# Moving W_out and the norms of the second token half beside the first half's down projection, and a convolution's LayerNorm across the first half's up projection

## The chip, the cores and the metric

The kernel runs as one program on all 8 cores of one Trainium2 chip. Each core computes 2,048 of the 16,384 tokens, and reads a window of 21 tiles of 128 tokens, because the attention and the convolution look back over 5 tiles. The metric is the device time of the slowest core in microseconds (us). Some executions of any 8-core program fall into a slower state, in which one die has a lower granted TensorE clock; all comparisons here use executions that were not in it, unless the text says so.

Engines are named as in the profile: PE is TensorE, DVE is VectorE, ACT is ScalarE, POOL is GpSimd, SP is SyncE (it mainly issues transfers). 

## The reference, cut to what matters

```python
u = rms_norm(x, norm_mix_pre)
a_val, a_gate, q, k, v = split(u @ w_in)              # 512 columns each
h = a_val * sigmoid(a_gate)
h = causal_depthwise_conv(h, dw_w, dw_b)              # width 31, 512 channels
conv_out = silu(layer_norm(h, ln_g, ln_b))
attn_out = chunked_band_attention(q, k, v, rel_bias)  # 8 heads, 576 keys per 64 queries
x = x + rms_norm(concat(conv_out, attn_out) @ w_out, norm_mix_post)
u = rms_norm(x, norm_ffn_pre)
h = causal_depthwise_conv(u @ w_up, w3, b3)           # width 3, 2 x 2816 columns
gate, val = split(h)
x = x + rms_norm((gelu(gate) * val) @ w_down, norm_ffn_post)
```

All inputs are float32. The kernel multiplies in bf16, so weights have to be cast on the chip.

## The kernel before

A core's program has these stages:

1. A prologue loads w_in as f32 through a ring of eight staging buffers (2 KB rows) and casts it on ACT and DVE; the first projections run.
2. Four attention "slots" (20 exponential steps each). The remaining projections are woven between the steps, and the first half of the convolution lies in the last slot.
3. The second half of the convolution, two LayerNorms, and W_out with its two norms for 17 tiles.
4. The gated FFN in two token halves, H0 and H1: 44 column blocks of the up projection (24 matmuls each), then 8 tiles of the down projection (44 matmuls each).

The convolution is done as matmuls with banded weights (`cwt`, 128 x 20,480 numbers that are mostly zeros), on data that is rearranged by a write to DRAM and a read back (`hd`). Its result is rearranged by a second round trip (`cd`). The instructions of stages 1 to 3 are ordered by a small list scheduler inside the kernel, which uses cost figures of its own; those of the FFN stay in program order on every engine.

The end of the program, with the stage that the change takes apart:

```python
def load_cwt():                      # called in slot 4: f32 in DRAM -> bf16 in SBUF
    for q in range(4):
        S.dma("pool", "cwt%d" % q, lambda q=q: pool.dma_start(out=cwt.ap[:, 8 * q:8 * q + 8, :, :]..., 
              in_=cwt_d[:, 8 * q * 640:(8 * q + 8) * 640]), writes=[cwt[q]], kb=2560, cast=True)

for g in (2, 3, 4, 5):
    slot(g)
load_wo()                            # 8 casting transfers, f32 in DRAM -> bf16 in SBUF
for _, f in conv_units(1):
    f()
conv_norm(0)                         # subtract, multiply (DVE), Silu (ACT), cd out and back, copies
conv_stats(1)
conv_norm(1)
for si in range(6):
    load_wup(si)
for t in range(17 + 5):              # W_out of tile t beside the norms of the tiles before it
    for lag, f in ((5, wo_tp), (4, wo_u), (3, wo_sq2), (2, wo_res), (1, wo_sq1), (0, wo_mm)):
        if 0 <= t - lag < 17:
            f(t - lag)
# ... cut ...
ffn()
```

The prologue's transfers:

```python
def load_w(dst, k, dcol, scol):
    i = wq_i[0] % 8                  # eight staging buffers
    wq_i[0] += 1
    st = wst[i]
    S.dma("sp", "wst%d" % i, lambda: sp.dma_start(out=st.ap, in_=w_in_d[k * 128:(k + 1) * 128, scol:scol + 512]),
          writes=[st], kb=256)
```

The softmax here doesn't subtract the row's maximum and nothing guards it: scores larger than these inputs give would overflow.

## Time and profile before

The median is 881.73 us (880.97 to 883.14). From the head of the profile: the span, and the busy share of PE and of the 16 DMA engines in 40 equal slices of the span (each digit counts tenths, a 9 is 90% or more).

```profile
span 882.3 us, 16351 instructions; the slowest of 8 cores (872.6 to 882.3 us)
...
PE   2898999999997728698999999999999999999996
...
DMA  8996411307977239685999999622399888810323
```

PE is busy 805.6 us in all, 91% of the span. Apart from the start, one gap stands out in its row: the digits 7 7 2 8 6 9 8, from about 265 to 420 us. The same by stage (busy time by window: start and end, length, busy us of each engine with its count of instructions, granted clock, share of the DMA engines, GB/s). The stages are prologue, slots, the stage of convolution, LayerNorm and W_out, then up-H0, down-H0, up-H1, down-H1:

```profile
core 5: us, PE busy (x) PEld busy (x) DVE busy (x) ACT busy (x) POOL busy (x), PEclk, DMA share, GB/s
0.00:80.00 80.00, 56.12 (x435) 29.14 (x436) 39.49 (x94) 42.50 (x80) 15.45 (x45) 0.96 0.85 269
80.00:276.00 196.00, 188.43 (x1828) 104.57 (x1828) 105.04 (x260) 110.98 (x138) 13.75 (x28) 1.00 0.51 77
276.00:407.50 131.50, 94.90 (x688) 58.11 (x689) 94.35 (x136) 94.76 (x191) 5.25 (x6) 0.86 0.62 165
407.50:566.60 159.10, 158.70 (x1081) 104.69 (x1082) 137.97 (x114) 119.46 (x121) 49.05 (x64) 0.99 1.03 120
566.60:646.50 79.90, 79.52 (x378) 36.62 (x376) 25.30 (x21) 12.29 (x20) 7.50 (x18) 1.00 0.28 93
646.50:798.40 151.90, 151.90 (x1033) 100.36 (x1034) 131.52 (x106) 111.09 (x107) 31.70 (x37) 1.00 0.75 74
798.40:882.30 83.90, 76.02 (x353) 34.22 (x350) 26.48 (x22) 11.99 (x19) 5.91 (x16) 0.98 0.28 94
```

The third stage has 131.5 us with 94.9 us of PE work, so 36.6 us of PE idle: that is about all that a better order of this stage can win, as long as PE leads in the stages that take its work over. The slots have 7.6 us of PE idle, and the up and down stages under 0.5 us, except for the 8 us tail.

The chain of waits (start, length, and what the chain passed through) goes through two round trips by way of DRAM, with the LayerNorm between them: `hd` out and back, 13.81 and 10.96 us from 251.78 us on, and then `cd`:

```profile
330.99 12.80 DMA cd<-big
343.91 11.21 DMA big<-cd
```

### The profile page before, as it was taken

The page shows a single profiled execution, that of the slowest core. Times are in us where ns is not written, and L with a number is a line of the kernel's source. Part 1 is how long each engine was busy: PE and PEld are TensorE (multiplying, and loading weights), DVE is VectorE, ACT ScalarE, POOL GpSimd, SP SyncE. Part 2 cuts the span into 40 slices and gives each one's busy share as a digit, 9 for nine tenths or more (in the row PEclk, how much of TensorE's full clock was granted, in tenths as well). Part 3 has the DMA queues.
Part 4 walks back from the last instruction along what each step waited for, and adds up shares of the span by engine and source line. Part 5 has one row for each costly group of instructions (what it writes and reads, how often), then busy time and mean ns, then how long its engine had stood idle before and what let it go on. Part 6 is the DMA issues. An engine that isn't in the chain of part 4 may idle for free.

```text
span 882.3 us, 16351 instructions; the slowest of 8 cores (872.6 to 882.3 us)
## 1 busy us (share of the span) xinstructions
PE 805.6 (91%) x5788; PEld 467.7 (53%) x5788; DVE 560.1 (63%) x750; ACT 503.1 (57%) x673; POOL 128.6 (15%) x213
## 2 busy tenths in 40 slices
PE   2898999999997728698999999999999999999996
PEld 1345445555476703355666666544466666664442
DVE  1666555545453674898988888922258888885232
ACT  3557655455571874798877777611157777773111
POOL 2211100000010020000333333101022222200000
PEclk9999999999998969799999999999999999999999
DMA  8996411307977239685999999622399888810323
GB/s 260 281 282 205 83 12 38 36 1 127 153 103 76 81 100 202 224 272 181 136 124 114 116 115 109 73 96 96 107 147 82 73 78 77 74 13 33 111 96 119
DMA packets 145507, 103.81 MB, mean 118 GB/s; under 512 B 116882, under 2 KB 124434, under 8 KB 144660
## 3 DMA queue, kind: packets, MB, share of 16 engines
q0 software_dynamic: 96704, 36.25, 38.2%
q1 hardware_dynamic: 48148, 65.93, 25.8%
q8 instruction: 47, 0.77, 0.4%
q10 hardware_dynamic: 576, 0.60, 0.3%
q14 instruction: 32, 0.26, 0.1%
HBM read 117.98 MB, written 21.02 MB: 158 GB/s over the span
## 4 chain that ended last, share of the span: by engine, by line
PE 77%; DMA 8%; DVE 6%; issue 4%; ACT 4%; POOL 1%; DVEq 0%; SPq 0%; ACTq 0%; POOLq 0%
PE ps L1036 34%; PE ps L1004 17%; PE ps L615 6%; PE ps L565 4%; PE ps L590 4%; PE ps L601 3%; DMA big<-w_in 2%; PE ps L711 2%; PE ps L746 2%; DMA hd<-big 2%; ACT big L870 2%; DMA cd<-big 1%; DMA big<-cd 1%; DMA big<-hd 1%; DVE big L946 1%
## 5 line engine op out<-in xcount | busy, mean ns | idle before, releaser
L1036 PE MATMUL ps<-big 128*128 128x344 bf16 (+1 forms) x2112 | 313.2, 309 | 1.2 <-DVE big L933 0.5
L1036 PEld LDWEIGHTS ps<-big 128*128 128x128 bf16 x2112 | 205.5, 97 | 108.0 <-issue 1.9
L1004 PE MATMUL ps<-big 128*128 128x512 bf16 x704 | 152.3, 379 | 0.0
L1041 ACT COPY big<-ps 128x1032 f32<-128x1032 f32 x88 | 89.6, 1018 | 82.5 <-DVE big L1045 56.3
L1045 DVE SCALAR_TENSOR_TENSOR big<-big 128x1026 f32<-128x1026 f32 x88 | 113.1, 1285 | 31.7 <-ACT big L1042 28.2
L990 POOL DMA_DIRECT2D big<-w_up x88 | 77.3, 881 | 339.6 <-PE ps L1036 185.6
L1048 DVE SCALAR_TENSOR_TENSOR big<-big 128x1026 f32<-128x1026 f32 x88 | 113.4, 1289 | 9.5 <-DVE big L933 0.4
L1004 PEld LDWEIGHTS ps<-big 128*128 128x128 bf16 x704 | 68.9, 98 | 82.8
L1042 ACT ACTIVATE big<-ps,big 128x1026 f32<-128x1026 f32 x88 | 106.8, 1213 | 0.0
L721 ACT ACTIVATE big<-ps 128x1024 bf16<-128x1024 f32 x80 | 81.8, 1023 | 35.5 <-PE ps L711 20.1
L1012 ACT ACTIVATE big<-ps 128x1024 bf16<-128x1024 f32 x16 | 16.4, 1024 | 129.8 <-PE ps L1004 129.8
L919 PE MATMUL ps<-big 128*128 128x512 bf16 (+1 forms) x272 | 63.9, 392 | 28.9 <-ACT big L870 18.1
L1016 DVE SCALAR_TENSOR_TENSOR big<-ps,big 128x1024 f32<-128x1024 f32 x16 | 20.5, 1284 | 105.7 <-POOL big L501 105.7
L615 PE MATMUL ps<-big 128*128 128x512 bf16 (+1 forms) x320 | 62.0, 339 | 0.5 <-DVE big L623 0.5
L919 PEld LDWEIGHTS ps<-big 128*128 128x128 bf16 (+1 forms) x272 | 26.3, 99 | 61.0 <-issue 33.7
L1059 DVE TENSOR_TENSOR big<-big 128x1026 bf16<-128x1026 bf16 x44 | 53.8, 1222 | 0.7 <-PE ps L1036 0.4
L565 PE MATMUL ps<-big 128*128 128x512 bf16 x168 | 43.5, 413 | 5.8 <-ACT big L493 4.8
L1056 ACT ACTIVATE big<-big 128x1026 bf16<-128x1026 f32 x44 | 46.5, 1057 | 0.4 <-DVE big L1048 0.4
L498 POOL TENSOR_SCALAR big<-big 128x1 f32<-128x1 f32 x37 | 7.7, 208 | 255.1 <-ACT big L1012 174.6
L590 PE MATMUL ps<-big 128*128 128x512 bf16 (+1 forms) x192 | 39.3, 354 | 1.0 <-DVE big L593 0.5
L615 PEld LDWEIGHTS ps<-big 128*128 128x128 bf16 x320 | 25.8, 97 | 26.3 <-issue 1.3
L727 DVE TENSOR_TENSOR big<-big 128x512 bf16<-128x512 bf16 (+1 forms) x80 | 29.4, 368 | 8.9 <-ACT big L721 4.3
(97 smaller groups left out, 796.6 us busy)
## 6 DMA issues: line engine op xcount, KB each, us to landing
big<-w_up POOLq DMA_DIRECT2D x88, 256.0 KB, 6.2
big<-xw SPq DMA_DIRECT2D x37, 512.0 KB, 6.1
big<-w_in SPq DMA_DIRECT2D x40, 256.0 KB, 8.5
h1s<-big SPq DMA_DIRECT2D x16, 512.0 KB, 3.7
big<-h1s SPq DMA_DIRECT2D x16, 512.0 KB, 4.5
out<-big SPq DMA_DIRECT2D x16, 512.0 KB, 3.1
big<-w_down POOLq DMA_DIRECT2D x22, 256.0 KB, 7.5
big<-cwt POOLq DMA_DIRECT2D x4, 1280.0 KB, 25.0
```

The costliest lines, as they stand in the source:

```text
L565: S.mm(lambda k=k: pe.matmul(b.ap, lhsT=ut.ap[:, k, j * 128:(j + 1) * 128], rhs=Wv.ap[:, k, :], start=(k == 0), stop=(k == 7)), reads=[ut[ ...
L590: S.mm(lambda k=k: pe.matmul(b.ap[:, :N], lhsT=Wk.ap[:, k, c * 128:(c + 1) * 128], rhs=ut.ap[:, k, :N], start=(k == 0), stop=(k == 7)), re ...
L615: S.mm(lambda k=k: pe.matmul(b.ap[:, :n], lhsT=Wa.ap[:, k, col:col + 128], rhs=ut.ap[:, k, n0:N], start=(k == 0), stop=(k == 7)), reads=ut ...
L721: S.op("act", lambda: act.activation(out=p_.ap, in_=s_.ap, func=AF.Exp), reads=[s_], writes=[p_, DH["exps"]], n=1024)
L919: S.mm(lambda k=k, half=half, l_=l_: pe.matmul(pp.ap[0:n, half, :], lhsT=l_, rhs=Wo.ap[:, k, half * 512:(half + 1) * 512], start=(k == 0), ...
L990: S.dma("pool", "wup%d" % (si % 8), lambda: pool.dma_start(out=wring[si % 8].ap, in_=w_up_v[:, :, cbk * 128:(cbk + 1) * 128]), reads=[coT[ ...
L1004: S.mm(lambda f=f, half=half, i=i, pdv=pdv: pe.matmul(pdv[:, half * 512:(half + 1) * 512], lhsT=actb.ap[:, f, i * 128:(i + 1) * 128], rhs= ...
L1036: S.mm(lambda k=k, t=t, n_=n_: pe.matmul(pu.ap[:, t, 0:n_], lhsT=wb.ap[:, k, :], rhs=u2T.ap[:, k, b0 + 342 * t:b0 + 342 * t + n_], start=( ...
L1041: S.op("act", lambda: act.copy(out=xs.ap, in_=pu.ap[:, :, 0:344]), reads=[pu], writes=[xs], n=1032)
L1042: S.op("act", lambda: act.activation(out=ta.ap, in_=pu.ap[:, :, 2:344], func=AF.Identity, scale=fdw.ap[:, cbk, 2:3], bias=fdw.ap[:, cbk, 3 ...
L1045: S.op("dve", lambda: dve.scalar_tensor_tensor(out=tB.ap, in0=xs.ap[:, :, 1:343], scalar=fdw.ap[:, cbk, 1:2], in1=ta.ap, op0=ALU.mult, op1 ...
L1048: S.op("dve", lambda: dve.scalar_tensor_tensor(out=ta.ap, in0=xs.ap[:, :, 0:342], scalar=fdw.ap[:, cbk, 0:1], in1=tB.ap, op0=ALU.mult, op1 ...
```

## The change

The intent is to dissolve the third stage. The W_out steps of the first token half and the first half's LayerNorm go into the attention slots. The second half's LayerNorm is spread in small pieces over the column blocks of up-H0, and the second half's W_out (tiles 9 to 16) goes beside down-H0, where DVE and ACT are idle. To free SBUF and to avoid table switches, the normalized activations `u2T` hold one token half only, Silu becomes a tanh form, Sqrt becomes integer and Newton steps on DVE, and the banded weights no longer stay in SBUF: they are cast once, DRAM to DRAM, and streamed twice through a ring of three pieces. W_out is cast DRAM to DRAM too. The core of the diff, cut:

```diff
+    cwb = nc.dram_tensor("cwb", [128, 32 * 5 * 128], BF16).ap()
+    wob = nc.dram_tensor("wob", [D, D], BF16).ap()
 ...
+        def cast_cwt(p):
+            S.dma("pool", "cwb%d" % p, lambda: pool.dma_start(out=cwb[:, p * 2560:(p + 1) * 2560], in_=cwt_d[:, p * 2560:(p + 1) * 2560]),
+                  writes=[DH["cwb"][p]], kb=1280, cast=True)
+        def load_cwt(i):
+            p = i % 8
+            S.dma("sp", "cwt%d" % (i % 3), ... out=cwr[i % 3], in_=cwb[:, p * 2560:(p + 1) * 2560], reads=[DH["cwb"][p]] ...)
+        def cast_wo():
+            for i in range(2):
+                S.dma("pool", "wob%d" % i, lambda i=i: pool.dma_start(out=wob[i * 512:(i + 1) * 512, :], in_=w_out_d[i * 512:(i + 1) * 512, :]),
+                      writes=[DH["wob"][i]], kb=2048, cast=True)
 ... in the prologue, behind the last load of w_in in program order:
+        for p in range(8):
+            cast_cwt(p)
+        cast_wo()
 ... in the loop of the up projection:
+                if H == 0:
+                    k, m = si // 4, si % 4
+                    if si < 32:
+                        (lambda: ln1.mul(k), lambda: [ln1.affine(k, i, "act") for i in (0, 1)],
+                         lambda: [ln1.affine(k, i, "act") for i in (2, 3)], lambda: ln1.tanh(k))[m]()
+                    if m == 0 and 0 < si <= 32:
+                        ln1.out(k - 1)
+                    if si == 32:
+                        ln1.cross()                      # cd out and back
+                    if si >= 37:
+                        for f in turns[2 * (si - 37):2 * (si - 36)]:
+                            f[1]()                       # ACT copies of what cd brought back
 ... in the down projection:
+            for i in range(8):
+                if H == 0 and i < 7:
+                    wo_mm(9 + i)
+                    wo_x(10 + i)
+                    if i:
+                        wo_tp(8 + i)
+                if i:
+                    epi(i - 1)
 ...
+                if H == 0:
+                    for f in (wo_ev, wo_res, wo_sq2, wo_u) if i < 7 else ():
+                        f(9 + i)
+                part(i, 0, 18)                           # 36 of the tile's 44 down matmuls
+                if H == 0 and i == 0:
+                    for f in turns[14:]:
+                        f[1]()
 ... the program's end:
-        load_wo()
-        for _, f in conv_units(1):
-            f()
-        conv_norm(0)
-        conv_stats(1)
-        conv_norm(1)
-        (the loop over 17 W_out tiles)
+        (woven into slots 2 to 5: conv_units, conv_stats, LayerNorm 0, W_out steps of tiles 0 to 8)
```

`cast_cwt` and `cast_wo` read inputs and write a DRAM tensor that nobody has touched, so they wait for nothing.

## The prediction

> **What bounds it now.** The table of engine busy time by 20 us windows (slowest core, span 882.3 us) shows four stages. (a) 0 to 80 us: DMA share 0.76 to 0.96, the loads of w_in set the pace. (b) 80 to about 276 us, attention woven with the projections: PE 97 to 100% busy, VectorE and ScalarE near 55%. (c) 276 to 407 us: PE busy only 5 to 14 us of 20 in four windows (300 to 360) and clock 0.71 to 0.86. The chain of waits names why: hd DMA out and back 13.8 + 11.0 us, LayerNorm on ACT/DVE, cd DMA 12.8 + 11.2 us, then W_out at 3.9 us a tile, 272 matmuls whose tile rate DVE and ACT set. (d) 407.5 to 882: two halves of up (159, 152 us) and down (76 us), PE-bound, plus a 8 us tail.
>
> **Removed.** Stage (c) as a stage. Its PE work from 276 on (rest of conv and its statistics about 25 us, W_out 16 x 3.45 us, transposes) moves elsewhere; the four exposed round trips, about 49 us, and the Silu/Sqrt table switches go.
>
> **Moved.** First-half W_out (9 steps, about 32 us of PE), conv 18 us and statistics 17 us go into the attention slots. I sum PE work there (projections 125, attention 45, conv, statistics, W_out) to about 237 us; DVE and ACT work, with the durations of before, to about 180 each. The slots stay PE-led; at 93% they last about 255 us, against 327 from 80 to 407. Up-H0 gains per four column blocks (13.9 us) about 1.3 us of DVE (87% to 97%) and 2.5 us of ACT (75% to 93%): I allow 4 us of PE stall. Down-H0 gains 8 x (3.45 + 0.45) = 31 us of PE, little else, since DVE (25% busy) and ACT (11%) are idle there. Up-H1, down-H1 and the tail stay 153 + 84.
>
> Sum: 80 + 255 + 4 (drain) + 157 + 109 + 1 + 153 + 84 = 843 us.
>
> **Added, and my main doubt.** The conv weights are now cast DRAM to DRAM (10.5 MB read) and W_out too (4.2 MB). These POOL DMAs depend on nothing, so they should be issued in the first 15 us, into the stage that is DMA-bound. The Trainium skill, "DMA: Bandwidth & Descriptors", section "Issuing engines are not separate DMA queues", says that all issuing engines share the same 16 DMA engines; this trace agrees: the hd write issued beside the cast of cwt at 202 us took about 36 us instead of a median 8.5. The cast of 5 MB there took about 35 us at DMA share above 0.8. Casts at the start can delay w_in by 0 to 40 us. I take 13 us as the middle of an uneven distribution: about 856 us.
>
> **Predicted: 856 us, 8 in 10 between 832 and 882; faster by over 2% 0.60, within 2% 0.35, slower 0.05.**
>
> **What would show it.** No window with PE under 50% after the prologue; first up matmul near 339 to 370 us; down-H0 near 107 us and down-H1 near 76; up-H0 not above 160; DMA share near 1 in the first 100 us and the first attention exp later than 80 us if my doubt is right; only about two activation table loads.
>
> **What would make it wrong.** Casts that share gently (then 840) or starve w_in fully (then 880). Fixed order: a late hd or cd round trip stalls PE in the slots. Only two generic PSUM banks serve W_out, its transposes and the projections. Tanh beside the tanh-GELU in up-H0: if they need different tables, each switch costs 1.28 us as measured here (skill page "ScalarE: Activation LUTs", section "Table sets", warns of switches), 16 times, about 20 us. DVE at 97% in up-H0 could slip more than 4 us.

## More of the kernel before

PE's own timeline shows where it stood still (start, length, line, instruction; brackets hold the idle time before an instruction and what ended it):

```profile
276.86 1.76 PE L819 MATMUL ps<-big 128*128 128x128 bf16 x15 [2.40 <-DMA big<-hd]
...
326.02 18.98 PE L919 MATMUL ps<-big 128*2 128x512 bf16 x80 [18.15 <-ACT big L870]
...
360.03 5.12 PE L919 MATMUL ps<-big 128*128 128x512 bf16 x16 [10.75 <-DVE big L933]
```

PE waited only 2.40 us for `hd`, because attention and convolution work ran beside that trip. The two long waits, 28.9 of the 36.6 us, are one that the profile puts down to ACT's Silu in the LayerNorm (line 870), and one that begins during the way back of `cd` (343.91 to 355.12 us) and ends after the copies of what it brought.

One more view, because the change meets it: the DMA queues in the first 80 us (packets, MB, share of the time of 16 engines) and the loads of w_in (count, KB each, median us from issue to landing). `q1` is SP's queue, `q0` is POOL's.

```profile
q1 hardware_dynamic: 10080, 21.25, 83.0%
q0 software_dynamic: 288, 0.07, 0.9%
...
big<-w_in SPq DMA_DIRECT2D x40, 256.0 KB, 8.5
```

The prologue is bound by SP's loads: they take 83% of all the DMA time that there is.

## The result, and the profile after

The kernel after takes 947.35 us (946.42 to 947.47), against 881.78 us for the kernel before in the same rounds: the ratio is 1.074, with a 95% interval of 1.072 to 1.076. It is 7.4% slower. (Ratios are the mean time of one kernel's fast runs over that of the other's in the same rounds, so they differ a little from the ratio of the medians.)

The head of the profile after, with the same lines:

```profile
span 946.3 us, 16431 instructions; the slowest of 8 cores (937.6 to 946.3 us)
...
PE   0031999989999998979999996999989999999996
...
DMA  8998984566037468427999998453329877840332
```

The gap in PE's row near 300 us is gone, as intended. A larger one has opened at the start: four slices of 23.7 us at 0, 0, 3 and 1 tenths. The windows by stage (prologue up to the first exponential of the attention, slots, up-H0, down-H0, up-H1, down-H1):

```profile
core 2: us, PE busy (x) PEld busy (x) DVE busy (x) ACT busy (x) POOL busy (x), PEclk, DMA share, GB/s
0.00:140.00 140.00, 56.41 (x388) 28.60 (x394) 34.17 (x78) 41.34 (x80) 21.03 (x50) 0.84 0.94 198
140.00:419.40 279.40, 256.22 (x2337) 152.08 (x2367) 167.68 (x342) 160.38 (x250) 49.53 (x119) 0.96 0.51 122
419.40:591.90 172.50, 162.58 (x1081) 105.69 (x1082) 141.33 (x126) 134.06 (x159) 48.96 (x63) 0.96 0.94 113
591.90:709.50 117.60, 111.14 (x557) 51.91 (x566) 56.59 (x62) 41.17 (x81) 18.35 (x41) 1.00 0.39 136
709.50:862.20 152.70, 152.65 (x1032) 101.05 (x1034) 131.61 (x106) 111.26 (x107) 32.41 (x37) 1.00 0.72 77
862.20:946.30 84.10, 75.61 (x345) 33.98 (x350) 26.45 (x22) 12.00 (x19) 6.33 (x16) 0.97 0.26 88
```

The difference of the two profiled spans, 64.0 us, splits exactly into three parts. In the kernel before, the first exponential starts at 78.2 us. (The slowest core is core 5 before and core 2 after.)

| stage | before | after | difference |
|---|---|---|---|
| up to the first exponential | 78.2 | 140.0 | +61.8 |
| from there to the first up matmul | 329.3 | 279.4 | -49.9 |
| FFN | 474.8 | 526.9 | +52.1 |

Single cores differ by some us within a run: before, their first exponential starts at 72.9 to 78.2 us. The medians of the eight cores give differences of +64.8, -52.9 and +50.0 us, so the picture is the same.

The prologue lost almost as much as the whole kernel did. But the table says a second thing: even with the old prologue, the moved work would have won 49.9 us in one place and paid 52.1 us in another. Of these 52.1 us, 31.6 are PE work that now stands in down-H0 (PE busy 111.14 against 79.52 us). Up-H0 got no matmuls (1,081 records in both), yet its PE busy time grew by 3.9 us: the granted clock was 0.91 and 0.75 in the stretches 419 to 440 and 560 to 580 us, the second of which holds a long wait, and 0.99 to 1.00 in the others. The rest is mostly waiting.

The chain of waits after begins with one long stretch of w_in loads and of SP's queue waiting to issue more loads (lines 500 and 485 issue those of w_in and x):

```profile
4.36 28.49 DMA big<-w_in
33.73 13.27 SPq L500
...
60.16 19.57 SPq L485
```

The DMA queues and issues of the first 80 us after:

```profile
q0 software_dynamic: 1517, 7.31, 77.4%
q1 hardware_dynamic: 1778, 4.30, 20.5%
...
big<-w_in SPq DMA_DIRECT2D x16, 256.0 KB, 40.1
```

Before, POOL's queue took 0.9% of the DMA time here and SP's 83%. Now POOL's takes 77.4% and SP's 20.5%. SP moved 4.30 MB instead of 21.25 MB, and a w_in load took 40.1 us instead of 8.5. POOL's part of the timeline (start, length, line, instruction) shows when the casts were issued:

```profile
3.12 1.58 POOL L846 DMA_DIRECT2D cwb<-cwt  x3
...
11.59 1.00 POOL L985 DMA_DIRECT2D wob<-w_out  x2
```

The timeline has all ten (five of them cut here) issued by 13 us, although they stand behind the loads of w_in in the program text. That text is only the order within an engine, and POOL had nothing else to do.

### The profile page after: what moved, and what is told of

Read it like the earlier page. It is cut to its first block, busy times and chain, and to the rows that moved or that the text cites. A ratio compares the mean times of both kernels' runs of the same rounds, so it can differ in the third digit from the quotient of the medians.

```text
span 946.3 us, 16431 instructions; the slowest of 8 cores (937.6 to 946.3 us)
## 1 busy us (share of the span) xinstructions
PE 814.6 (86%) x5731; PEld 473.3 (50%) x5788; DVE 557.8 (59%) x734; ACT 500.2 (53%) x692; POOL 176.6 (19%) x326
## 4 chain that ended last, share of the span: by engine, by line
PE 59%; DVE 12%; DMA 9%; issue 7%; SPq 6%; ACT 4%; POOL 2%; DVEq 0%; ACTq 0%; POOLq 0%
PE ps L1183 23%; PE ps L1112 10%; PE ps L638 6%; PE ps L610 3%; SPq L500 3%; DMA big<-w_in 3%; PE ps L585 3%; PE ps L1028 3%; SPq L485 3%; DVE big L1192 3%; DVE big L1195 2%; PE ps L624 2%; PE ps L865 2%; PE ps L734 2%; DMA big<-xw 2%
## 5 line engine op out<-in xcount | busy, mean ns | idle before, releaser
L1183 PE MATMUL ps<-big 128*128 128x344 bf16 (+1 forms) x2112 | 318.0, 312 | 9.1 <-ACT big L1189 8.6
L1183 PEld LDWEIGHTS ps<-big 128*128 128x128 bf16 x2112 | 207.5, 99 | 118.7 <-issue 11.3
L1112 PEld LDWEIGHTS ps<-big 128*128 128x128 bf16 x704 | 68.0, 97 | 81.7
L745 ACT ACTIVATE big<-ps 128x1024 bf16<-128x1024 f32 x80 | 80.5, 1024 | 44.0 <-PE ps L770 22.1
L518 POOL TENSOR_SCALAR big<-big 128x1 f32<-128x1 f32 (+1 forms) x54 | 16.0, 296 | 292.1 <-ACT big L537 130.1
L638 PE MATMUL ps<-big 128*128 128x512 bf16 (+1 forms) x311 | 61.6, 344 | 2.4 <-DVE big L646 1.4
L1028 PE MATMUL ps<-big 128*128 128x512 bf16 (+1 forms) x262 | 61.4, 381 | 2.6 <-DVE big L1045 1.1
L521 POOL TENSOR_TENSOR big<-big 128x1 f32<-128x1 f32 x71 | 48.6, 685 | 54.6 <-DVE big L1045 47.2
L547 PE MATMUL ps<-big 128*128 128x128 bf16 x168 | 14.8, 240 | 48.4 <-DVE big L593 25.0
L757 POOL MEMSET big<- 64x128 bf16 x64 | 14.0, 218 | 170.7 <-ACT big L745 133.1
L585 PEld LDWEIGHTS ps<-big 128*128 128x128 bf16 x168 | 17.2, 107 | 55.9 <-issue 41.8
```

The lines of the kernel that those rows point to most:

```text
L585: S.mm(lambda k=k: pe.matmul(b.ap, lhsT=ut.ap[:, k, j * 128:(j + 1) * 128], rhs=Wv.ap[:, k, :], start=(k == 0), stop=(k == 7)), reads=[ut[ ...
L638: S.mm(lambda k=k: pe.matmul(b.ap[:, :n], lhsT=Wa.ap[:, k, col:col + 128], rhs=ut.ap[:, k, n0:N], start=(k == 0), stop=(k == 7)), reads=ut ...
L745: S.op("act", lambda: act.activation(out=p_.ap, in_=s_.ap, func=AF.Exp), reads=[s_], writes=[p_], n=1024)
L1028: S.mm(lambda k=k, half=half, l_=l_, b=b: pe.matmul(b.ap[0:n], lhsT=l_, rhs=Wo.ap[:, k, half * 512:(half + 1) * 512], start=(k == 4), stop ...
L1112: S.mm(lambda f=f, half=half, i=i: pe.matmul((PU[1] if i % 2 else PD).ap[:, half, :], lhsT=actb[f].ap[:, i * 128:(i + 1) * 128], rhs=Wd[f] ...
L1183: S.mm(lambda k=k, t=t, n_=n_: pe.matmul(pu.ap[:, t, 0:n_], lhsT=wb.ap[:, k, :], rhs=u2T.ap[:, k, 342 * t:342 * t + n_], start=(k == 0), s ...
```

## The experiments

The first theory was that the casts are the whole loss: they hold the DMA engines while w_in should arrive. The rival was that the loss is made of the fixed order in the FFN and of busier slots, with the casts a side matter.

### e1: the kernel before, with the ten casts and nothing else

The casts write two DRAM tensors that nothing reads.

```diff
--- before
+        for p in range(8):
+            S.dma("pool", "cwb%d" % p, lambda p=p: pool.dma_start(out=cwb[:, p * 2560:(p + 1) * 2560], in_=cwt_d[:, p * 2560:(p + 1) * 2560]),
+                  writes=[DH["cwb"][p]], kb=1280, cast=True)
+        for i in range(2):
+            S.dma("pool", "wob%d" % i, lambda i=i: pool.dma_start(out=wob[i * 512:(i + 1) * 512, :], in_=w_out_d[i * 512:(i + 1) * 512, :]),
+                  writes=[DH["wob"][i]], kb=2048, cast=True)
         late = [Wa[(7, 0)]]
```

> The kernel before plus only the ten early DRAM-to-DRAM casts, whose results nobody reads. Theory A (the casts hold the DMA engines for about 63 us in a stage that is bound by DMA): first attention exp moves from 78 us to about 135 to 142 us and the total from 882 to about 940 to 950 us. Theory B (the new order and buffers of the prologue delay it, the casts slip in between): total within 10 us of 882.

Measured: 947.8 and 948.3 us, ratio 1.0756 (1.0722 to 1.0789). Four of its six runs fell into the slow state, the profiled one among them, so of its trace only the start and the undisturbed cores are used. On the slowest core the first exponential began at 143.5 us, and the DMA queues of the first 80 us read like those of the kernel after:

```profile
q0 software_dynamic: 1516, 7.28, 76.2%
q1 hardware_dynamic: 1778, 4.30, 22.8%
```

Cores 0 to 3, whose die was not slowed, start their first exponential at 139.1 to 141.0 us and take 473.2 to 474.9 us for the FFN, as in the kernel before, so the delay arises in the prologue and nothing is added later.

What follows: the casts alone, added to the old kernel, cost about 66 us, which is all of the loss. The rest of the change is then worth about nothing (947.35 against some 948 us), which agrees with the table above (-49.9 and +52.1). Neither theory was the whole of it: the casts make the loss, and the fixed order and the moved work eat the gain.

### e2: the kernel after, with the casts held back until w_in is loaded

```diff
--- after
         for p in range(8):
-            cast_cwt(p)
-        cast_wo()
         late = [Wa[(7, 0)]]
+        for p in range(8):
+            cast_cwt(p, late)        # reads=late: waits for the last cast weight of w_in
+        cast_wo(late)
```

> The changed kernel with the ten casts held back until the last w_in weight is in place (about 72 us). Theory A: first exp back at 78 to 85 us; but the casts then take their 63 us of DMA time inside the first attention slot, so the conv weights come at about 140 us and the hd round trip is slow: total 885 to 915 us. Theory B: first exp stays near 140 us, total above 940 us.

Measured: 938.41 us, ratio 1.0665 (1.0596 to 1.0735). The first exponential came at 76.6 us again, but the first up matmul only at 413.2 us: of 63 us won in the prologue, 6 were left. The total lies between the two ranges that were expected. The timelines of ACT and PE show one place where most of the 63 us went:

```profile
146.85 1.06 ACT L537 ACTIVATE big<-big 128x1024 bf16<-128x1024 f32 x1 [53.66 <-DMA big<-xw]
...
148.63 5.04 PE L638 MATMUL ps<-big 128*128 128x512 bf16 x15 [51.76 <-ACT big L642]
```

PE stood still for 51.76 us in the middle of the first slot. It waited for ACT (line 642), and ACT, which works in program order, stood for 53.66 us before the norm of a tile of x (line 537) whose load had not landed. That load (512 KB) was issued at 87.06 us and took 59.7 us; the 32 KB write of `hd`, issued just before it at 86.25 us, took 59.4 us. In this stretch (72 to 145 us) POOL's queue took 86.8% of the DMA time. So the casts take their time from whatever transfers run beside them; to move them only chooses the victim.

### e3: the kernel after, casting directly to SBUF

The ring is filled straight from the f32 weights by casting transfers, as the kernel before did, so the weights are read twice; W_out likewise. There is no DRAM-to-DRAM transfer.

```diff
--- after
-        for p in range(8):
-            cast_cwt(p)
-        cast_wo()
 ... in load_cwt:
-            S.dma("sp", ... in_=cwb[:, p * 2560:(p + 1) * 2560]), reads=[DH["cwb"][p]], ...)
+            S.dma("pool", ... in_=cwt_d[:, p * 2560:(p + 1) * 2560]), ... kb=1280, cast=True)
 ... in load_wo:
-                S.dma("sp", ... in_=wob[k * 128:(k + 1) * 128, :]), reads=[DH["wob"][k // 4]], ...)
+                S.dma("pool", ... in_=w_out_d[k * 128:(k + 1) * 128, :]), ... kb=512, cast=True)
```

> The changed kernel without the staging in DRAM: conv weights and W_out are cast straight into SBUF, each conv weight twice, when their buffers come free. Theory A: first exp at 78 to 85 us, total 880 to 900 us, so no better than before, because 20 us in the slots, 15 in the first up and 8 in the first down stay lost. Theory B: total above 940 us.

Measured: 913.8 us (three runs), ratio 1.0359 (1.0317 to 1.0401). The first exponential came at 74.4 us and the first up matmul at 390.1 us. The total is above the 880 to 900 us that were expected: the slots became longer, which the expectation had not counted. Half of the loss is gone without any DRAM-to-DRAM cast; what is left is the FFN, 523.4 us on the profiled span and so 48.6 more than before, and slots of 315.7 us, in which POOL's queue took 30.2% of the DMA time (74 to 314 us), most of it to cast the mostly empty weights twice. That the casts made the slots longer was not tested apart; the longest single wait of PE in them is 11.9 us.

### e4 and e5: the two waits in the FFN

The kernel after has two waits that come from the fixed order. At the end of up-H0, ACT's copies of what `cd` brings back ("turns") stand in ACT's order before the data is there. ACT waits, and PE waits for ACT to drain PSUM. The timeline of the kernel after, ACT and PE:

```profile
571.74 1.15 ACT L974 COPY big<-big 128x256 bf16<-128x256 bf16 x2 [8.62 <-DMA big<-cd]
...
575.05 16.83 PE L1183 MATMUL ps<-big 128*128 128x344 bf16 x96 [8.12 <-ACT big L1189]
```

In down-H0 every tile's transposes (`wo_tp`, line 1084) stand before the tile's own down matmuls and wait for a chain of norms (ACT, POOL, DVE line 1074) of the tile before, while ACT cannot go on before it has copied those transposes out of PSUM (line 1090), which holds up the squares of the next tile's norms behind it:

```profile
635.46 1.29 DVE L1074 SCALAR_TENSOR_TENSOR big<-big 128x1024 bf16<-128x1024 f32 x1 [2.92 <-POOL big L521]
...
636.89 0.61 PE L1084 MATMUL ps<-big 128*128 128x128 bf16 x8 [0.96 <-DVE big L1074]
...
637.59 1.01 ACT L1090 COPY big<-ps 128x1024 bf16<-128x1024 bf16 x1 [3.75 <-PE ps L1084]
```

The loop closes over PE, DVE and ACT in 14.4 us per tile, where PE has 13.4 us of work.

e4 put the copies later, across the down tiles 0, 2 and 4, and was not run: the check refused it, with 66 values that are no numbers; the buffer that the copies read starts at the same SBUF address as one of the output tiles (129732), which is written from tile 1 on (this is read from the program, not tested).

> The changed kernel with two orders mended in the FFN: only 4 of the 16 turns of conv output stay in the first up (at its end), 12 go into the first down; and each transpose of W_out comes behind the down projection of its tile, not in front of it. Theory C (the first up lost 8 us to a wait of ACT on the cd read and 2 to 4 us to ACT overload by the turns, the first down 7 us to an in-order loop over transpose, ACT and DVE): first up 172 to 160-163 us, first down 117.6 to 109-111 us, total about 931 us. Rival D (DVE at 95% in the first up and the added PE work in the first down set those times): both stages within 2 us, total 945 us or more.

e5 keeps the copies within the buffer's life: 4 of the 16 in the last two column blocks, 12 in down tile 0. And the transposes go behind the tile's first 36 down matmuls.

```diff
--- after
-                    if si >= 37:
-                        for f in turns[2 * (si - 37):2 * (si - 36)]:
+                    if si >= 42:
+                        for f in turns[2 * (si - 42):2 * (si - 41)]:
 ...
-                    for f in turns[14:]:
+                    for f in turns[4:]:
 ...
-                    if i:
-                        wo_tp(8 + i)
 ...
                 part(i, 0, 18)
+                if H == 0 and 0 < i < 7:
+                    wo_tp(8 + i)
```

> The changed kernel, casts untouched, with two orders mended in the FFN: 4 of the 16 turns of conv output stay at the end of the first up, 12 go into the first tile of the first down; each transpose of W_out comes behind the down projection of its tile, not in front of it. Theory C (the first up lost 8 us to ACT waiting for the cd read and a few to the turns, the first down 7 us to an in-order loop over transpose, ACT and DVE): first up from 172 to 160-164 us, first down from 118 to 109-112 us, total 929 to 934 us. Rival D (DVE at 95% in the first up, and the PE work added to the first down, set those times): both within 2 us, total 945 us or more.

Measured: 939.89 us, ratio 1.0647 (1.0622 to 1.0673). Up-H0 fell from 172.5 to 166.8 us, and down-H0 from 117.6 to 113.5 us with a period of 13.4 us per tile, PE's own work. But the step from up-H0 to down-H0 now held a wait, for the first four copies, which were issued so late that they themselves ended late:

```profile
587.19 5.08 PE L1028 MATMUL ps<-big 128*128 128x512 bf16 x12 [4.86 <-ACT big L974]
```

The wait comes before the first down matmul, so the 166.8 us of up-H0, taken up to that matmul, contain it. Both stages and the total ended above the ranges expected (160 to 164, 109 to 112, 929 to 934 us). So the two waits are real, and together worth about 7.5 us as mended here, after the loss of 4.9 us to a new wait. They are about a ninth of the loss, not its main part.

### e6 and e7: no casts at all

If the casts are too dear in any place, the weights must come in some other way. `cwt` holds each of its numbers among fifteen zeros. e6 sends the numbers without the zeros (1,280 per partition instead of 20,480, and a 16 x 16 mask), lets DVE multiply them out in slot 2, and stores the bf16 pieces to the same DRAM tensor; the ring is unchanged. W_out is cast straight to SBUF, as before the change. No arithmetic moves to the host; the same numbers arrive in another layout.

```diff
--- after
-    cwt_d = dr("cwt", [128, 32 * 5 * 128])
+    cws_d = dr("cws", [128, 32 * 5 * 8])
+    msk_d = dr("msk", [128, 16])
 ...
+        def build_cwt(p):
+            t = cst[p % 2]
+            for a in range(0, 160, 40):
+                S.op("dve", lambda a=a: dve.tensor_tensor(
+                    out=t.ap[:, a:a + 40, :], in0=cws.ap[:, p * 160 + a:p * 160 + a + 40].unsqueeze(2).to_broadcast([128, 40, 16]),
+                    in1=mskb.ap.unsqueeze(1).to_broadcast([128, 40, 16]), op=ALU.mult), ...)
+            S.dma("sp", ... out=cwb[:, p * 2560:(p + 1) * 2560], in_=t ...)
```

> The changed kernel without any early cast: the banded conv weights are built on VectorE from their 1/16 of nonzero numbers (the host passes the same numbers without the zeros), stored to DRAM by the hardware queue in the first attention slot, and W_out is cast straight into SBUF. Theory A (the early casts cost 62 us and nothing else in the prologue does): first exp at 75 to 82 us, first up matmul at 355 to 370 us, total 883 to 897 us, so the rest of the change is worth nothing to -2%. Theory B: first exp near 140 us, total above 940 us. Should the slots turn out limited by DVE, 22 us more of it would push the first up past 370 us.

Measured: 890.62 us, ratio 1.0089 (1.0021 to 1.0158). First exponential 72.3 us, first up matmul 362.1 us. The casts are out of the way and 57 us are back. The slots became 10.4 us longer than in the kernel after (289.8 against 279.4); it would fit that the building, 32 DVE instructions in the first slot and the wait of the convolution for them, costs about that much.

e7 adds e5's two orders, and moves the attention's memsets, which the change had sent to POOL, back to DVE.

```diff
--- e6
+        (the edits of e5)
-        S.op("pool", lambda m0=m0: pool.memset(p_...
+        S.op("dve", lambda m0=m0: dve.memset(p_...
```

> e6 with the FFN orders of e5, and with the attention memsets back on VectorE. If the stage effects add: e6 minus 15 to 18 us from the FFN, 866 to 880 us in all, faster than before by 0.5 to 2%. Memsets: if the hand-over DVE to POOL to PE (DVE waits 15.7 us for POOL memsets in the slots) delays the attention chain, the time from first exp to first up is 3 to 10 us shorter than in e6; if PE sets the slots, it is equal within 2 us.

Measured: 879.93 us, ratio 0.9978 (0.9924 to 1.0032): a tie with the kernel before. The FFN begins 45.7 us earlier than there (361.8 against 407.5). Up-H0 is 7 us longer and down-H0 34 us longer, so little remains. The memsets made no clear difference: the slots went from 289.8 to 288.2 us on the slowest cores, while the cores of one run spread over 284.2 to 290.5 us in e6.

### e8 and e9: two attempts on the slots

e8 gives every second building piece to POOL and puts the first four copies at column blocks 40 and 41. e9 also moves the first convolution later in its slot, so that PE should not wait for it.

```diff
--- e7
-                    if si >= 42:
-                        for f in turns[2 * (si - 42):2 * (si - 41)]:
+                    if si in (40, 41):
+                        for f in turns[2 * (si - 40):2 * (si - 39)]:
 ...
-                S.op("dve", lambda a=a: dve.tensor_tensor(
+                e, en = (("dve", dve), ("pool", pool))[p % 2]
+                S.op(e, lambda a=a, en=en: en.tensor_tensor(
--- e9 also
-                         (conv_units(0), 0.6, 0.85), ... (one(lambda: conv_stats(0)), 0.9, 1.0)]
+                         (conv_units(0), 0.72, 0.95), ... (one(lambda: conv_stats(0)), 0.98, 1.0)]
```

> e7 with two small changes: the first four turns of conv output come two column blocks earlier in the first up, so that they are done when the first W_out matmul of the first down wants them (e7 waited 4.5 us there), and every second piece of the conv weights is built on POOL, since DVE was 80% busy in the first attention slot of e7 and POOL 13%. Expected: wait before the first down gone (-4 us), time from first exp to first up from 288 to 280-286 us; total 868 to 876 us, faster than before by 0.7 to 1.6%. If POOL work slows DVE beside it, the slots stay at 288 us and the total at 875 us.

> e8 with the first conv 10% of a slot later, so that the hd round trip it waits for (4.1 us in e7) has landed, and its statistics later with it. Theory: waits of PE on DMA in the slots fall by 4 us and the total to 864 to 872 us. Rival: the LayerNorm chain of the first half is the tighter limit, so a later conv moves its cd round trip and W_out back and the total rises by 3 to 10 us.

Measured: e8 876.73 us, ratio 0.9941 (0.9910 to 0.9971); e9 877.74 us, ratio 0.9958 (0.9931 to 0.9985), no different from e8. Both missed their expectations: e8's slots were to fall to 280 to 286 us, and e9 was to take 864 to 872 us. In e8 the slots took 296.9 us on the slowest core; the median of its cores is 288.9 us, against 284.9 in e7, with overlapping spreads, so the split did not shorten them, and how much it lengthened them is not clear. The groups of instructions show one thing against the split (line, engine, operation, shapes, count; busy us and mean ns; idle time before and what ended it):

```profile
L853 POOL TENSOR_TENSOR big<-big 128x640 bf16<-128x640 f32 x16 | 24.4, 1556 | 9.8 <-DMA cwb<-big 7.9 <-DMA big<-msk 1.8
L853 DVE TENSOR_TENSOR big<-big 128x640 bf16<-128x640 f32 x16 | 16.9, 1106 | 2.7 <-DMA cwb<-big 2.2 <-DMA big<-msk 0.5
```

A piece takes 1,556 ns on POOL, and DVE's own pieces took 1,106 ns beside it, against 810 ns when DVE worked alone (e12 below).

### e10 and e11: what in a cast is dear

e10 is e1 with only the two casts of W_out. e11 is e1 with all ten casts, but with destinations cut so that a packet is 640 bytes (conv weights) or 512 bytes (W_out) instead of 5,120 and 32,768.

```diff
--- e1, for e10
-        for p in range(8):
-            S.dma("pool", "cwb%d" % p, ...)
--- e1, for e11
-    cwb = nc.dram_tensor("cwb", [128, 32 * 5 * 128], BF16).ap()
-    wob = nc.dram_tensor("wob", [D, D], BF16).ap()
+    cwb = nc.dram_tensor("cwb", [64, 128, 320], BF16).ap()
+    wob = nc.dram_tensor("wob", [4, D, 256], BF16).ap()
```

> The kernel before plus only the two early casts of W_out (in the trace of e1 their 32 KB packets took 18 us of all 16 DMA engines, those of the conv weights 43). Theory A (delay = DMA engine time of the casts): first exp from 78 to 94-100 us, total 898 to 904 us. Rival (a fixed cost of any early cast on that queue, or of its order): near 940 us, or under 888 us.

> e1 with the same ten casts and bytes, but rows cut to 320 and 256 numbers, so that packets have 640 and 512 bytes in place of 5,120 and 32,768. Theory A1 (each DMA engine takes packets of the two queues in turn, so the queue with the larger packets gets the larger share): w_in gets about half of the time, first exp between 100 and 130 us where e1 had 143.5. Theory A2 (the casts come first whatever their packets, or the sum of work alone counts): first exp at 140 us or later, total 940 us or more.

Measured, e10: 901.8 us (two runs), ratio 1.0227 (1.0195 to 1.0259); first exponential at 94.5 us, 16.3 later than before. POOL's queue in its first 80 us:

```profile
q0 software_dynamic: 384, 2.16, 23.6%
```

The casts of W_out are 64 packets of 32 KB, each 4.51 us long, which is 64 x 4.51 / 16 = 18 us of all 16 engines. The delay was 16.3 us on the slowest cores and 19.7 us in the medians of the eight. In the trace of e1 the conv weights' casts are 1,024 packets of 672 ns, which is 43 us of 16 engines. Both together are 61 us, and the kernel after starts its first exponential 61.8 us late (64.8 us in the medians). So the size of the loss is plain DMA work: in this stage, which is bound by the DMA engines, each us of cast was about a us of delay, within a tenth. The 5 MB of `cwt` did not look like 43 us of work, because a plain 2,048-byte packet of w_in takes 107 ns in the trace of before, 19 bytes per ns, where a casting DRAM-to-DRAM packet of 5,120 bytes makes 7.6. (These are the bytes written; a cast from f32 to bf16 reads twice as many.) The kernel before casts the same `cwt` straight into SBUF, and there it took 31.4 us of 16 engines (57.0% of the stretch from 195 to 250 us), in slots that PE leads: so the change made this cast dearer, and put it where DMA is the limit.

Measured, e11: 939.5 us (two runs), ratio 1.0655 (1.0622 to 1.0688); first exponential at 124.8 us, against 143.5 in e1. Its queues in the first 80 us:

```profile
q1 hardware_dynamic: 6514, 13.11, 60.6%
q0 software_dynamic: 6047, 3.70, 40.6%
```

With small packets POOL's queue gets 40.6% instead of 76.2%, though it holds the same transfers. In this pair of runs the size of the packets set how the two queues shared the engines. The first exponential is as theory A1 expected. But the total moved by only 8 us: the cast work that was held back ran into the first slot instead (the DMA share is 1.01 from 125 to 152 us, and the slots took 336.1 us against 327.8 in e1, medians of the cores). The work is the cost, and the share only dates it.

### e12 and e13: the best version

e12 is e7 with the first four copies at column blocks 40 and 41 (as in e8, but with all building on DVE). e13 also makes bf16 copies of the numbers and the mask first, in the hope that DVE multiplies bf16 faster.

```diff
--- e7, for e12
-                    if si >= 42:
-                        for f in turns[2 * (si - 42):2 * (si - 41)]:
+                    if si in (40, 41):
+                        for f in turns[2 * (si - 40):2 * (si - 39)]:
--- e12, for e13
+        S.op("dve", lambda: dve.tensor_copy(out=cwh.ap, in_=cws.ap), ...)
+        S.op("dve", lambda: dve.tensor_copy(out=mskh.ap, in_=mskb.ap), ...)
-                    in0=cws.ap..., in1=mskb.ap...
+                    in0=cwh.ap..., in1=mskh.ap...
```

> e8 without the building on POOL (its POOL pieces took 1.56 us each beside 0.81 on DVE, and its time from first exp to first up rose from 288 to 297 us), so e7 with only the four turns earlier. Expected: the 4.5 us wait before the first down gone, slots 286-290 us, total 873 to 877 us, ratio 0.990 to 0.996.

> e12 with the conv weights built from bf16 copies: if DVE is faster on bf16 with repeated operands (the attention multiply of 512 bf16 took 0.42 us where 512 f32 took 0.69), each build step falls from 0.81 to 0.4-0.6 us, DVE gives back 7 to 12 us in the first attention slot, and the total is 3 to 8 us below e12. If the repeated operand keeps DVE at its slow rate, both are equal within 2 us.

Measured: e12 873.66 us, ratio 0.9910 (0.9889 to 0.9930); e13 871.95 us (five runs), ratio 0.9889 (0.9840 to 0.9939). What e13 hoped for did not come: the building runs no faster in bf16, and the two are equal within 2 us, the other outcome that was named. The groups of e12 and of e13:

```profile
L852 DVE TENSOR_TENSOR big<-big 128x640 bf16<-128x640 f32 x32 | 24.4, 810 | 2.8 <-DMA cwb<-big 2.6
```

```profile
L854 DVE TENSOR_TENSOR big<-big 128x640 bf16<-128x640 bf16 x32 | 24.4, 808 | 2.6 <-DMA cwb<-big 2.6
```

Both are about 1% faster than the kernel before, with an interval that excludes equality. e12's stages, from its profile: first exponential 72.7 us, first up matmul 362.5, down-H0 524.3, up-H1 635.7, end 872.4. Its FFN takes 509.9 us, 35.1 more than before, and 33.5 of that is PE busy time, 31.5 in down-H0, to which the work was moved. The long waits in the FFN are gone: up-H0 has 1.7 us of PE idle left, down-H0 0.4.

## Why the prediction was wrong, point by point

It said 856 us and "faster"; the result was 947.35 us, far outside its range. Its sum, term by term (the profiled span was 946.3 us; the two add up to a miss of 90.3 us):

| term | predicted | measured | miss |
|---|---|---|---|
| prologue with casts | 80 + 13 | 140.0 | +47.0 |
| slots and drain | 255 + 4 | 279.4 | +20.4 |
| up-H0 | 157 | 172.5 | +15.5 |
| down-H0 | 109 + 1 | 117.6 | +7.6 |
| up-H1, down-H1, tail | 153 + 84 | 236.8 | -0.2 |

**The step that failed: "I take 13 us as the middle of an uneven distribution".** The mechanism was right: the casts depend on nothing, go out in the first 15 us, and share the DMA engines with the loads of w_in. The Trainium skill, "DMA: Bandwidth & Descriptors", section "Issuing engines are not separate DMA queues", says that transfers of all issuing engines run on the same 16 DMA engines; the trace agrees (POOL's queue 77.4%, SP's 20.5% of those engines). The size was wrong. The prediction had costed the cast of 5 MB at about 35 us from the trace of before, left W_out's casts without a figure of their own, and then averaged between "shares gently" and "starves". In a stage with a DMA share of 0.85 there was little to share: the delay had to be nearly the whole DMA time of the casts, measured at 61 us from their packets, and the whole range of "0 to 40 us" was too low. e1, e10 and the packet times show this. (The 35 us were those of a cast into SBUF; into DRAM it took 43.) Even "starve w_in fully (then 880)" was 67 us under the result. It is not the only error that reversed the sign: with the casts alone mis-sized the sum is 843 + 60 = 903 us, and with the other terms alone mis-sized it is 856 + 43 = 899 us. Either is slower than the kernel before.

**"I sum PE work there ... to about 237 us".** PE was busy 256.2 us in the slots, and at the measured 92% (the prediction had 93%) that makes 279.4. The groups of the slots of the kernel after show which terms were missing:

```profile
L770 PE MATMUL ps<-big 128*128 128x65 bf16 x632 | 31.5, 197 | 3.1 <-DVE big L781 2.2 <-DVE big L751 0.8
L734 PE MATMUL ps<-big 64*128 64x128 bf16 (+3 forms) x252 | 25.6, 315 | 5.1 <-ACT big L745 5.1
...
L547 PE MATMUL ps<-big 128*128 128x128 bf16 x96 | 7.7, 226 | 0.8 <-DVE big L705 0.4 <-DVE big L793 0.3
L1084 PE MATMUL ps<-big 128*128 128x128 bf16 (+1 forms) x72 | 6.1, 233 | 1.2 <-DVE big L1042 0.5 <-DVE big L1045 0.4 <-DVE big L1074 0.2
L789 PE MATMUL ps<-big 128*128 128x128 bf16 x48 | 4.8, 225 | 2.0 <-DVE big L793 1.6 <-DVE big L874 0.2
```

The attention (lines 734 and 770) takes 57.1 us where the sum had 45, and the transposes (547, 1084 and 789), 18.6 us, were not in it at all. (Groups overlap: in this stage they add up to 279.7 us, 23.5 more than PE's busy time. So the 12.1 and 18.6 us cannot be set one for one against the 19.2 us that the sum lacked; the groups show which terms were short, not by how much each.) The table of windows would have given it without a sum of parts: 188.43 + 94.90 us of PE work from 80 to 407.5 us, less the 31 us that go to down-H0, is 252.

**"I allow 4 us of PE stall" in up-H0.** The allowance was for DVE and ACT being fuller. What cost most was order: ACT stood for 8.62 us before data that `cd` had not yet brought, and PE for 8.12 us behind it; besides, the same matmuls were busy 3.9 us longer, at a lower granted clock. The warning "a late hd or cd round trip stalls PE" was in the prediction, but for the slots and with no number. e5 and e12 mend it: 172.5, 166.8 and 161.8 us.

**Down-H0.** The PE work was right (31 us predicted, 31.6 measured). The order made each tile 14.4 instead of 13.4 us long; with the transposes behind the first down matmuls, down-H0 takes 113.5 us in e5 (after one wait of 4.9 us, counted in up-H0), and 111.4 us in e12.

**"Removed: stage (c) as a stage" as a gain.** The prediction called four exposed round trips of about 49 us a gain, but for `hd` PE itself had waited 2.40 us. It did move the stage's PE work and not drop it; still its sum without casts, 843 us, lies 39.3 us under the old span, more than the 36.6 us of PE idle that there was to win in the stage. The PE work came back in stages that are PE-bound. Without the casts and with the waits mended, e12 wins 9.9 us on the profiled spans: the prologue -5.5, the slots -39.5 and the FFN +35.1 (in the medians of the cores -1.8, -45.1 and +34.4, so the prologue's share is mostly a difference of cores).

**What was right.** Up-H1, down-H1 and the tail did not change. The DMA share is near 1 in the first 100 us and the first exponential is late, as the prediction said for the case that its doubt was right. No slice after the longer prologue has PE under 50%. And tanh beside the tanh-GELU costs no table switch: the kernel after has two table loads in all, 1.28 us each, against seven before. The Trainium skill, "ScalarE: Activation LUTs", section "Table sets", warns of switches between sets; this pair of functions showed none.

**What stays open.** The slots of e12 take 289.8 us with 259.1 us of PE work, so about 31 us of idle time are left in them. The largest part that the trace names is PE waiting for the exponentials on ACT (line 749), 10.9 us in 8 waits, against 5.1 us in the kernel after; `hd` and `cwb` transfers add 6.7 us. e9 (a later convolution) and the memsets of e7 did not find them; that the building on DVE holds some 10 us of it fits e6 but was not shown apart.

## What to carry to other kernels

A transfer that depended on nothing was issued here as soon as its engine was free (all ten casts by 13 us), so "behind it in the program" gives no protection; before adding one, count its packets times the time of a packet over 16 engines, and add all of that where the stage is bound by DMA. Work that is moved from a stage with idle PE into a stage bound by PE is paid there in full: the most to be won is the idle time of the old place, read from the busy time by window, and the busy time is also a better sum of the work than a list of parts. In code that runs in program order, put an instruction that waits for a round trip behind work that can go on without it, and check where the wait goes next.

## What the Trainium skill lacked or had wrong

- "DMA: Bandwidth & Descriptors" has no cost for a casting DRAM-to-DRAM transfer. Here a 5,120-byte packet took 672 ns and a 32,768-byte packet 4.5 us (7.6 and 7.3 bytes written per ns of one engine), against 107 ns for a plain 2,048-byte packet to SBUF (19 bytes per ns).
- The same page, section "Queues, rings and completion order", says that a DMA engine turns between queues packet by packet. The runs agree in direction, but the page does not draw the consequence that these runs show, that the queue with the larger packets got the larger share (packets as the profile counts them): 76.2% of the engines at 5,120 and 32,768 bytes, 40.6% at 640 and 512 bytes, against the same loads of w_in.
- "ScalarE: Activation LUTs", section "Table sets", gives about 2.7 us for a switch in its example; the page's section "What ACT_TABLE_LOAD costs" splits this into about 1,283 ns of load and about 1,380 ns of drain. Each load in the traces of before and after took 1,283 ns, but no such drain is seen beside the load at 292.27 us of the kernel before: ACT's next instruction starts 1.58 us after the end of the one in front of the load. The section does not say that tanh and the tanh-GELU run beside one another without a switch, as they did here (two loads in the whole kernel).
